# The FFN down projection of a one-core decoder trunk, as four full passes and as seven half-size block products

## The chip, the cores and the metric

The kernel runs on one core of one Trainium2 chip. The metric is the time of one execution on the device, in microseconds (us). The time before is the median of three runs; beside it one execution was recorded by the hardware profiler.

## What is computed

One layer of a decoder trunk on 1024 tokens of width 1024, in float32: a mixing sub-layer with three branches, then a feed-forward sub-layer with a causal convolution of three taps, then a norm. The change is in the last part:

```python
def reference(x, ...):
    h = rms_norm(x, norm_mix[l]);  proj = h @ w_in[l]          # 1024 -> 7184 columns
    ...                                                        # branches a, b, c; gates; w_o
    x = x + merged @ w_o[l]
    h = rms_norm(x, norm_ffn[l])
    a = causal_dwconv(h @ ffn_w_up[l], ffn_conv_w[l]) + ffn_conv_b[l]    # 1024 -> 2 x 2816
    gate, val = jnp.split(a, 2, axis=-1)
    x = x + (jax.nn.silu(gate) * val) @ ffn_w_down[l]                    # 2816 -> 1024
    return rms_norm(x, norm_final)
```

## The kernel before

Every large product runs on TensorE in three matmuls for one: each float32 operand is split into a rounded part `hi` (a ScalarE cast) and a rest `lo` (a subtraction on VectorE or GpSimd), and hi x hi, hi x lo and lo x hi are added up in a PSUM bank of 128x512. In the tiles' names `whi`, `wlo` are weights, `dh`, `dl` the operands of the down projection, `hl` weight operands of the block products, `ah`, `al` their activation operands.

The stages follow one another: norm and first products; the projections (24 blocks); the linear attention and the three branches; `w_o`; the up projection (22 blocks, one for each 128 columns of gate and of value); the down projection with the final norm.

The projections and the up projection already use block products (`Stage`): a block's 2x2 product takes seven products instead of eight, in the order `B11, T1, T2, B22, T3, B21, T4`. The T weights are sums of weight quarters, the S activations sums of activation quarters. A product is 12 matmuls. `prep_right` makes a product's weight operand (line 405 to 416) seven products ahead of its matmuls; `step` moves a finished product from PSUM to the block's tiles `zg` and `zu`, by a ScalarE copy (441 to 445, 453) or a VectorE add (447 to 451). Blocks interleave by one product: the T4 of a block comes after the B11 of the next. The up stage begins with a fill of six blocks (`FILL`), for which B11 and B21 come first.

Side work runs in lanes. `later(delay, step, lane)` puts a step at the end of a lane's queue; `tick` is called after every 3 matmuls (4 ticks a product) and lets each lane's first step go when its delay has passed since the one before. `store_later(delay, out_, in_)` issues a store so many ticks later on SP's queue, `flush` and `flush_stores` run what is left. SP and TensorE keep the order of the program. ScalarE, VectorE and GpSimd are put in order by a planner, which works with modelled times, except in regions marked `manual_schedule`, where they keep the program's order too. All large tiles come from one pool of 52 buffers (`NB`).

After a block's T4, `post_up` applies the taps (ScalarE line 1045, VectorE 1046 and 1048), Silu (1055) and the product with the value half (1057), and stores the tile `tap` to `actd` in HBM.

The down projection runs four passes, for each half of the output columns (`ch`) and of the tokens (`hf`). A pass goes over 11 pairs of blocks (`fp`): an activation pair is loaded from `actd` (`act_pair`, lines 1076 to 1079), weights `dn` by `weights` when `hf` is 0 (162 to 169), and four row blocks take 6 matmuls each. The first two passes also load the residual from `x2d` (`load_residual`) and transpose it on TensorE into `otf` (`residual`, line 1108). `finish` (1121 to 1131) adds the PSUM bank to the residual, sums squares, multiplies with the norm's weight and, in the second half of the columns, scales the rows, which `put_outs` stores. The last three pairs of the last pass run row block by row block.

Of the kernel before, what the change touches and what calls it, by code (L numbers as in the profile page):

```python
# [10 lines left out]
F32 = mybir.dt.float32  # L11
# [5 lines left out]
P = 128  # L17
# [40 lines left out]
def host_layout(inp):  # L58
# [17 lines left out]
    for name in plan():  # L76
# [18 lines left out]
        elif name[:2] == "dn":  # L95
            r, c = int(name[3:]) * 2 * P, int(name[2]) * HALF
            parts.append(kt(w_dn[r:r + 2 * P, c:c + HALF]))
# [22 lines left out]
def trunk_kernel(ctx: ExitStack, tc: tile.TileContext, wst, vec, xt, x, ws, wal, rows, out):  # L120
# [471 lines left out]

    PFILL = 0
# [152 lines left out]

    proj.run(proj_ahead, 2 * PFILL)
# [323 lines left out]
    NP = NF // 2  # L1071

    def act_pair(fp, hf):
        raw = B((P, 2, HALF), name="araw")
        s = slice(hf * HALF, hf * HALF + HALF)
        nc.sync.dma_start(out=raw, in_=actd[2 * fp:2 * fp + 2, :, s].rearrange("f p t -> p f t"))
# [3 lines left out]
        return hi, lo  # L1080

    wdn = {}
    passes = [(0, 0), (0, 1), (1, 0), (1, 1)]
    jobs = [(ch, hf, fp) for ch, hf in passes for fp in range(NP)]
    got = {}

    def fetch(i):
        if i >= len(jobs) or i in got:
            return
        ch, hf, fp = jobs[i]  # L1090
        if hf == 0:
            wdn[ch, fp] = tuple(t.rearrange("p (f c) -> p f c", c=HALF) for t in weights(f"dn{ch}{fp}", 0))
        got[i] = act_pair(fp, hf)
# [24 lines left out]
    def finish(ch, c, ps):  # L1118
        s = slice(ch * HALF, ch * HALF + HALF)
        ot, st = otf[c], fss[:, c]  # L1120
        nc.vector.tensor_tensor(ot[:, s], ps, ot[:, s], op=ALU.add)
        nc.scalar.activation(ps, ot[:, s], AF.Square, accum_out=st[:, ch:ch + 1])
        nc.vector.tensor_tensor(ot[:, s], ot[:, s], nfin[:, s], op=ALU.mult)
        if ch == 0:
            return
# [3 lines left out]
        nc.scalar.activation(ot[:, 0:HALF], ot[:, 0:HALF], AF.Copy, scale=st[:, 2:3])  # L1129
        outs_.append((out[rows_, 0:HALF], ot[:, 0:HALF]))  # L1130
        nc.vector.tensor_scalar(ot[:, HALF:D], ot[:, HALF:D], st[:, 2:3], None, op0=ALU.mult)
        outs_.append((out[rows_, HALF:D], ot[:, HALF:D]))
# [43 lines left out]
    flush_stores()  # L1176

    LAST = 3
    i = 0
    for n, (ch, hf) in enumerate(passes):  # L1180
        banks = [PB() for _ in range(4)]

        def down(j, c, fp):
            w, a = wdn[ch, fp], got[j]
            cs = slice(c * P, c * P + P)
            for q in range(2):
                hi, lo = a[0][:, q, cs], a[1][:, q, cs]
                for e, (l, r) in enumerate(((hi, w[0][:, q]), (hi, w[1][:, q]), (lo, w[0][:, q]))):
                    mm(banks[c], l, r, fp == 0 and q == 0 and e == 0, fp == NP - 1 and q == 1 and e == 2)

        tail = LAST if n == len(passes) - 1 else 0
        for fp in range(NP - tail):
            for a in range(4):
                fetch(i + fp + a)
            if fp == 2:
                put_outs()
            for c in range(4):
                down(i + fp, c, fp)
            got.pop(i + fp)
            if ch == 0 and fp in (1, 3, 5, 7):  # L1200
                load_residual(hf * 4 + fp // 2)
            if ch == 0 and fp in (4, 6, 8, 10):
                residual(hf * 4 + fp // 2 - 2)
        for fp in range(NP - tail, NP):
            fetch(i + fp)
        for c in range(4):
            for fp in range(NP - tail, NP):
                down(i + fp, c, fp)
            finish(ch, hf * 4 + c, banks[c])
            if tail:  # L1210
                put_outs()
        i += NP

# [22 lines left out]
```

## Time and profile before

| | |
|---|---|
| median of 3 runs | 1573.9 us (1572.3 to 1575.32) |
| the profiled execution | 1574.62 us |
| its span, first to last instruction | 1572.9 us |
| TensorE busy | 1530.4 us, 97% of the span |
| mean granted clock of TensorE | 0.986 of full speed |
| VectorE, ScalarE, GpSimd busy | 949.1, 663.2, 404.1 us |
| moved by DMA | 184.08 MB |

The span is that of the profiled execution; the 1.7 us between it and the execution's time lie before the first and behind the last instruction. "Busy" counts time in which an engine has an instruction under way. PE is TensorE, PEld its weight loads, DVE VectorE, ACT ScalarE, POOL GpSimd, SP the queue that issues all DMAs. L424 is line 424 of the kernel.

### The profile page before, as it was taken

To read this page: it belongs to the slowest core of one execution; us is meant where nothing else is said; L and a number is where in the kernel's file an instruction comes from. 1 tells how busy PE (TensorE), PEld (TensorE's weight loads), DVE (VectorE), ACT (ScalarE), POOL (GpSimd) and SP (SyncE) were. 2 spreads that over 40 slices of the span, in tenths; PEclk is the share of its full clock that TensorE was granted. 3 is DMA by queue.
4 is the path that set the end of the run, shared out by engine and by line. 5 is a ranking of instruction groups with operands and counts; after the bars stand their busy time and mean duration, and the time that the engine had idled before them with its cause. 6 is when DMAs were issued, how large, how long until landed. Compare 5 with 4: busy or idle time off the path is not lost.

```text
span 1572.9 us, 18223 instructions
## 1 busy us (share of the span) xinstructions
PE 1530.4 (97%) x7096; PEld 1263.9 (80%) x7096; DVE 949.1 (60%) x1093; ACT 663.2 (42%) x1017; POOL 404.1 (26%) x236
## 2 busy tenths in 40 slices
PE   8899999999999999997999999999999999999998
PEld 8787778888888887875888878888888887888886
DVE  7858776644444442546532698987777775343652
ACT  6634643443343441145122355555444444333341
POOL 5202222222222212015333521222222223302600
PEclk9999999999999999998999999999999999999999
DMA  7223022223323254234424412222222224754341
GB/s 286 94 88 120 36 73 82 93 108 114 114 108 107 81 199 189 91 124 149 145 81 138 157 51 84 94 94 91 92 86 80 81 87 133 275 186 149 121 147 54
DMA packets 74645, 184.08 MB, mean 117 GB/s; under 512 B 6192, under 2 KB 22720, under 8 KB 74560
## 3 DMA queue, kind: packets, MB, share of 16 engines
q1 hardware_dynamic: 74560, 182.93, 33.4%
q8 instruction: 55, 0.90, 0.2%
q14 instruction: 30, 0.25, 0.0%
HBM read 140.96 MB, written 41.94 MB: 116 GB/s over the span
## 4 chain that ended last, share of the span: by engine, by line
PE 83%; issue 7%; DVE 5%; ACT 3%; POOL 1%; DMA 1%; SPq 0%; POOLq 0%; DVEq 0%; ACTq 0%
PE pb L424 48%; PE pb L142 29%; PE pss L142 3%; PE pss L424 2%; DVE hl L416 1%; POOL wlo L169 1%; ACT hl L414 0%; PE pss L1108 0%; DVE al L997 0%; DMA xr<-in_x 0%; DVE raw L409 0%; DVE raw L405 0%; DVE x L1009 0%; DVE raw L411 0%; DVE x L1029 0%
## 5 line engine op out<-in xcount | busy, mean ns | idle before, releaser
L424 PE MATMUL pb<-ah,hl 128*128 128x512 f32 x1856 | 583.3, 391 | 10.1 <-ACT zu L443 5.7
L424 PEld LDWEIGHTS pb<-ah,hl 128*128 128x128 f32 x1856 | 349.9, 189 | 87.7 <-ACT zu L443 6.9
L416 POOL TENSOR_TENSOR hl<-raw,hl 128x512 fp32r<-128x512 f32 x138 | 210.4, 1539 | 651.2 <-ACT hl L414 465.6
L424 PE MATMUL pb<-al,hl 128*128 128x512 f32 x928 | 362.5, 391 | 0.0
L416 DVE TENSOR_TENSOR hl<-raw,hl 128x512 fp32r<-128x512 f32 x184 | 179.0, 981 | 121.1 <-ACT hl L414 118.6
L414 ACT CAST hl<-raw 128x512 fp32r<-128x512 f32 x322 | 186.4, 618 | 125.0 <-DVE raw L407 88.6
L424 PEld LDWEIGHTS pb<-al,hl 128*128 128x128 f32 x928 | 175.0, 189 | 35.9
L169 POOL TENSOR_TENSOR wlo<-raw,whi 128x1024 fp32r<-128x1024 f32 (+1 forms) x50 | 128.7, 2586 | 267.5 <-ACT whi L167 239.3
L424 PE MATMUL pb<-h_hi,hl 128*128 128x512 f32 x576 | 181.7, 389 | 0.0
L142 PE MATMUL pb<-whi,dh 128*128 128x512 f32 x352 | 137.7, 391 | 0.0
L142 PE MATMUL pb<-whi,dl 128*128 128x512 f32 x352 | 137.0, 389 | 0.0
L142 PE MATMUL pb<-wlo,dh 128*128 128x512 f32 x352 | 137.0, 389 | 0.0
L142 PE MATMUL pb<-hi,wlo 128*128 128x512 f32 x320 | 127.1, 397 | 4.1 <-POOL wlo L169 4.1
L142 PE MATMUL pb<-hi,whi 128*128 128x512 f32 x320 | 129.8, 406 | 0.0
L142 PE MATMUL pb<-lo,whi 128*128 128x512 f32 x320 | 127.1, 397 | 0.3 <-DVE lo L229 0.3
L424 PEld LDWEIGHTS pb<-h_hi,hl 128*128 128x128 f32 x576 | 108.1, 188 | 23.2 <-issue 0.8
L1079 DVE TENSOR_TENSOR dl<-araw,dh 128x1024 fp32r<-128x1024 f32 x44 | 82.1, 1895 | 60.5 <-ACT dh L1078 59.1
L424 PE MATMUL pb<-h_lo,hl 128*128 128x512 f32 x288 | 112.0, 389 | 0.0
L142 PEld LDWEIGHTS pb<-whi,dl 128*128 128x128 f32 x352 | 66.1, 188 | 13.9
L142 PEld LDWEIGHTS pb<-whi,dh 128*128 128x128 f32 x352 | 66.1, 188 | 13.5
L142 PEld LDWEIGHTS pb<-wlo,dh 128*128 128x128 f32 x352 | 66.1, 188 | 13.3
L142 PEld LDWEIGHTS pb<-hi,wlo 128*128 128x128 f32 x320 | 61.5, 192 | 17.9 <-POOL wlo L169 4.6
(204 smaller groups left out, 2041.5 us busy)
## 6 DMA issues: line engine op xcount, KB each, us to landing
raw<-in_wst SPq DMA_DIRECT2D x138, 512.0 KB, 4.4
araw<-actd SPq DMA_DIRECT2D x44, 512.0 KB, 5.2
ld<-spd SPq DMA_DIRECT2D x42, 512.0 KB, 4.1
actd<-tap SPq DMA_DIRECT2D x22, 512.0 KB, 2.9
spd<-zg SPq DMA_DIRECT2D x17, 512.0 KB, 2.6
spd<-zu SPq DMA_DIRECT2D x17, 512.0 KB, 3.5
xr<-in_x SPq DMA_DIRECT2D x8, 512.0 KB, 7.7
x<-in_xt SPq DMA_DIRECT2D x16, 256.0 KB, 3.9
```

The costliest lines, as they stand in the source:

```text
L142: nc.tensor.matmul(o, lhsT=l, rhs=r, start=start, stop=stop)
L169: eng.tensor_tensor(lo, raw, f(hi), op=ALU.subtract)
L414: nc.scalar.copy(w[:, 0], t)
L416: eng.tensor_tensor(w[:, 1], t, f(w)[:, 0], op=ALU.subtract)
L424: nc.tensor.matmul(ps, lhsT=l, rhs=r, start=first and k == 0 and i == 0, stop=k == 3 and i == 2, skip_group_check=True)
L1079: nc.vector.tensor_tensor(lo, raw, f(hi), op=ALU.subtract)
```

## The change

The down projection becomes seven block products over all 11 pairs, in the order named above, each with one half of the tokens, one half of the columns and one block of 128 of each pair. Its T weights and S activations are made ahead and pass through HBM. `down_sums` loads the two weight blocks of a pair during the projections, makes four sums on VectorE and stores them to `tsd`; all 22 of its steps are queued in lane 2 before the projections begin. In the up stage, Silu and the product behind it move from `post_up` into `silu`, ten ticks later in a lane of its own (lane 3); every second one calls `act_sums`, four sums on VectorE stored to `ssd`. In the down stage a step loads an activation half and a weight half (`load_step`, six steps ahead), casts and subtracts both at once (`fetch`, four steps ahead), and runs 12 matmuls. VectorE takes all of these subtractions; GpSimd has none. Finished banks are added to the residual after the first step of the next product (`after`), and the whole stage keeps the program's order on all engines. The residual tiles are loaded and transposed within the first product, and the last stores of the up stage wait until its fourth step. The weights lie in HBM as `da` and `db`, one block of 128 rows each.

```diff
-    for ch in range(2):
-        names += [f"dn{ch}{fp}" for fp in range(NF // 2)]
+    for fp in range(NF // 2):
+        names += [f"da{fp}", f"db{fp}"]
...
-    def flush(lanes=(0, 1, 2)):
+    def flush(lanes=(0, 1, 3, 2)):
...
+    tsd = tc.dram_tile([NP, 4, P, HALF], F32, name="tsd")
+    ssd = tc.dram_tile([NP, 4, P, HALF], F32, name="ssd")
...
+    def down_sums(fp):
+        q = {}
+        def fetch_():
+            q["a"], q["b"] = B(name="dqa"), B(name="dqb")
+            for e in "ab":
+                o_ = offs[f"d{e}{fp}"]
+                nc.sync.dma_start(out=q[e], in_=wst[o_:o_ + P * T].rearrange("(p n) -> p n", p=P))
+        def sums():
+            t, u = B((P, 2, HALF), name="dt12"), B((P, 2, HALF), name="dt34")
+            w11, w12, w22, w21 = q["a"][:, left], q["a"][:, rite], q["b"][:, left], q["b"][:, rite]
+            for o_, l, r in ((t[:, 0], w12, w11), (t[:, 1], w22, t[:, 0]), (u[:, 0], w22, w12), (u[:, 1], w21, t[:, 1])):
+                nc.vector.tensor_tensor(o_, l, r, op=ALU.subtract)
+            for i, z in enumerate((t, u)):
+                store_later(16 + 4 * i, tsd[fp, 2 * i:2 * i + 2].rearrange("s p n -> p s n"), z)
+        later(24, fetch_, lane=2)
+        later(16, sums, lane=2)
...
+    for fp in range(NP):
+        down_sums(fp)
     proj.run(proj_ahead, 2 * PFILL)
...
             tg = taps(zg, fi)
-            nc.scalar.activation(tg, tg, AF.Silu)
             tu = taps(zu, NF + fi)
-            nc.vector.tensor_tensor(tg, tg, tu, op=ALU.mult)
-            store_later(14, actd[fi], tg)
+            later(10, lambda: silu(fi, tg, tu), lane=3)
...
+    def silu(fi, tg, tu):
+        nc.scalar.activation(tg, tg, AF.Silu)
+        nc.vector.tensor_tensor(tg, tg, tu, op=ALU.mult)
+        store_later(14 if fi < NF - 2 else 26, actd[fi], tg)
+        pend[fi] = tg
+        if fi % 2:
+            act_sums(fi // 2)
+    def act_sums(fp):
+        one, two = pend.pop(2 * fp), pend.pop(2 * fp + 1)
+        a11, a12, a21, a22 = one[:, left], two[:, left], one[:, rite], two[:, rite]
+        t, u = B((P, 2, HALF), name="as12"), B((P, 2, HALF), name="as34")
+        def put(i, z):
+            store_later(14, ssd[fp, 2 * i:2 * i + 2].rearrange("s p n -> p s n"), z)
+        def first():
+            nc.vector.tensor_tensor(t[:, 0], a21, a22, op=ALU.add)
+            nc.vector.tensor_tensor(t[:, 1], t[:, 0], a11, op=ALU.subtract)
+            put(0, t)
+        def second():
+            nc.vector.tensor_tensor(u[:, 0], a11, a21, op=ALU.subtract)
+            nc.vector.tensor_tensor(u[:, 1], a12, t[:, 1], op=ALU.subtract)
+            put(1, u)
+        later(6, first, lane=2)
+        later(4, second, lane=2)
...
+    jobs = [(m, fp) for m in ORDER for fp in range(NP)]
+    def load_step(i):
+        if i >= len(jobs) or i in raws_:
+            return
+        m, fp = jobs[i]
+        raws_[i] = raw = B((P, 2, HALF), name="araw")
+        a = LEFT[m]
+        if a[0] == "S":
+            nc.sync.dma_start(out=raw[:, 0], in_=ssd[fp, int(a[1]) - 1])
+        else:
+            s = left if a[1] == "1" else rite
+            nc.sync.dma_start(out=raw[:, 0], in_=actd[2 * fp + int(a[2]) - 1, :, s])
+        if m[0] == "T":
+            nc.sync.dma_start(out=raw[:, 1], in_=tsd[fp, int(m[1]) - 1])
+        else:
+            load_down(raw[:, 1], {"B11": f"da{fp}", "B22": f"db{fp}", "B21": f"db{fp}"}[m], int(m == "B21"))
+    def fetch(i):
+        if i >= len(jobs) or i in got:
+            return
+        raw = raws_[i]
         hi, lo = B((P, 2, HALF), F32R, "dh"), B((P, 2, HALF), F32R, "dl")
         nc.scalar.copy(hi, raw)
         nc.vector.tensor_tensor(lo, raw, f(hi), op=ALU.subtract)
+        got[i] = hi, lo
...
-        if n - 1 - i in (8, 6, 4, 2):
-            fetch((9 - n + i) // 2)
+        if n - 1 - i in (14, 10, 7, 5, 3, 1):
+            j = len(raws_)
+            load_step(j)
+            later(9, lambda: fetch(j), lane=1)
+        if n - 1 - i in (4, 2):
+            load_residual(len(xcs))
...
     up.run(up_ahead)
     flush()
-    flush_stores()
...
+    def down(i, c, first):
+        m, fp = jobs[i]
+        hi, lo = got[i]
+        cs = slice(c * P, c * P + P)
+        ps = banks["a" if BANK[m] == "a" else "c"][c]
+        for e, (l, r) in enumerate(((hi, hi), (hi, lo), (lo, hi))):
+            nc.tensor.matmul(ps, lhsT=l[:, 0, cs], rhs=r[:, 1], start=first and fp == 0 and e == 0,
+                             stop=fp == NP - 1 and e == 2, skip_group_check=True)
+    def after(m, c):
+        hf, ch, whole = {"B11": (0, 0, 0), "T1": (1, 1, 0), "T2": (0, 1, 0), "B22": (0, 1, 1), "T3": (1, 1, 1),
+                         "B21": (0, 0, 1), "T4": (1, 0, 1)}[m]
+        add(ch, hf * 4 + c, banks["a" if BANK[m] == "a" else "c"][c])
+        if whole:
+            finish(ch, hf * 4 + c)
+    with tc.manual_schedule(engines={ET.Activation, ET.DVE, ET.Pool}):
+        for n, m in enumerate(ORDER):
+            if m == "T1":
+                banks["c"] = [PB(), PB(), PSS(), PSS()]
+            first = m in ("B11", "T1", "B21")
+            i = n * NP
+            tail = LAST if m == "T4" else 0
+            for fp in range(NP - tail):
+                for a in range(DEPTH + 1):
+                    load_step(i + fp + a)
+                for a in range(DEPTH - 1):
+                    fetch(i + fp + a)
+                if fp in (2, 5):
+                    put_outs()
+                for c in range(4):
+                    down(i + fp, c, first)
+                    if n and fp == 0:
+                        after(ORDER[n - 1], c)
+                got.pop(i + fp)
+                if n == 0:
+                    if fp == 3:
+                        flush_stores()
+                    if 1 <= fp < 7:
+                        load_residual(fp + 1)
+                    if 2 <= fp < 10:
+                        residual(fp - 2)
+        i = n * NP
         for fp in range(NP - tail, NP):
             fetch(i + fp)
         for c in range(4):
             for fp in range(NP - tail, NP):
+                down(i + fp, c, False)
+            after("T4", c)
+            put_outs()
```

`add` adds a bank to `otf`; `finish` keeps the rest of what it did, with its squares written to a buffer `junk` in place of the PSUM bank, and scales the rows after the first half of the columns, which is now the last. `DEPTH` is 6 and `LAST` 3.

## Rows read from the trace of the kernel before

**Rows 1.** The page's head: busy us, share of the span, instructions.

```profile
PE 1530.4 (97%) x7096; PEld 1263.9 (80%) x7096; DVE 949.1 (60%) x1093; ACT 663.2 (42%) x1017; POOL 404.1 (26%) x236
```

**Rows 2.** The page's chain that ended last, by engine.

```profile
PE 83%; issue 7%; DVE 5%; ACT 3%; POOL 1%; DMA 1%; SPq 0%; POOLq 0%; DVEq 0%; ACTq 0%
```

**Rows 3.** Windows of 40 us: busy of PE, PEld, DVE, ACT, POOL; clock; DMA.

```profile
240.00:280.00 40.00, 40.00 (x178) 33.10 (x178) 26.05 (x29) 12.21 (x23) 11.27 (x8) 1.00 0.31 105
...
920.00:960.00 40.00, 37.53 (x156) 29.90 (x155) 37.98 (x41) 23.69 (x34) 13.17 (x6) 0.96 0.17 53
...
1160.00:1200.00 40.00, 40.00 (x178) 33.11 (x177) 32.08 (x34) 18.65 (x28) 10.21 (x7) 1.00 0.23 80
...
1280.00:1320.00 40.00, 38.08 (x161) 31.01 (x160) 27.70 (x28) 21.80 (x29) 13.80 (x6) 0.96 0.39 132
...
1520.00:1560.00 40.00, 40.00 (x178) 33.14 (x177) 9.54 (x14) 6.98 (x11) 0.00 (x0) 1.00 0.12 45
```

**Rows 4.** The chain in order of time, down stage: start, length, what.

```profile
1345.57 0.87 PE pss L1108 x8
...
1445.78 119.71 PE pb L142 x528
```

**Rows 5.** Groups by line and form: busy us, mean ns, idle before.

```profile
L1078 ACT CAST dh<-araw 128x1024 fp32r<-128x1024 f32 x44 | 45.2, 1048 | 14.2 <-DMA araw<-actd 13.2 <-PE pb L142 0.6 <-DMA raw<-in_wst 0.3
...
L169 POOL TENSOR_TENSOR wlo<-raw,whi 128x1024 fp32r<-128x1024 f32 x46 | 122.7, 2678 | 260.8 <-ACT whi L167 239.3 <-PE pb L142 21.3
...
L405 DVE TENSOR_TENSOR raw<-raw 128x512 f32<-128x512 f32 x46 | 31.5, 685 | 49.4 <-POOL hl L416 47.9 <-DMA raw<-in_wst 1.5
...
L411 DVE TENSOR_TENSOR raw<-raw 128x512 f32<-128x512 f32 x46 | 58.0, 1262 | 0.8
```

**Rows 6.** One tile, activations of the down stage: ns min/median/max.

```profile
L1079 DVE TENSOR_TENSOR dl<-araw,dh x44: 1214/1226/3432, 1295.3 to 1524.9; 128x1024 fp32r<-128x1024 f32 x44
```

**Rows 7.** Windows of 5 us at the stage's edge, columns as in rows 3.

```profile
1300.00:1305.00 5.00, 3.66 (x17) 2.69 (x15) 2.79 (x3) 5.00 (x7) 3.65 (x2) 1.00 0.76 213
1305.00:1310.00 5.00, 4.42 (x12) 3.49 (x13) 5.00 (x5) 1.85 (x4) 0.00 (x0) 0.66 0.26 101
...
1335.00:1340.00 5.00, 5.00 (x24) 4.14 (x23) 2.66 (x2) 2.59 (x4) 2.93 (x2) 1.00 1.05 413
```

**Rows 8.** VectorE's timeline at the end: start us, us, operation, idle before.

```profile
1565.51 0.69 DVE L1121 TENSOR_TENSOR ot<-pb,ot 128x512 f32<-128x512 f32 x1 [0.78 <-PE pb L142]
...
1568.32 0.49 DVE L1131 TENSOR_SCALAR ot<-ot,fss 128x512 f32<-128x512 f32 x1
```

**Rows 9.** SP's timeline in the projections and behind the up stage.

```profile
129.16 52.75 SPq L162 DMA_DIRECT2D raw<-in_wst  x6
...
1311.62 16.04 SPq L200 DMA_DIRECT2D actd<-tap  x2
```

**Rows 10.** One tile, the residual: a load's time from issue to landing.

```profile
DMA to landing us min/median/max: 3.7/6.9/10.8
```

**Rows 11.** The chain in order of time at the end of the up stage.

```profile
1300.38 0.95 ACT whi L167
...
1302.79 2.27 ACT tap L1045 x2
```

**Rows 12.** Windows of 10 us early in the projections, columns as in rows 3.

```profile
170.00:180.00 10.00, 7.35 (x26) 5.76 (x25) 8.00 (x10) 6.89 (x11) 2.52 (x2) 0.83 0.00 0
...
190.00:200.00 10.00, 8.62 (x39) 6.79 (x37) 8.99 (x8) 6.37 (x10) 4.24 (x4) 1.00 0.28 106
```

**Rows 13.** Groups by line on VectorE, four up blocks (1160 to 1236).

```profile
L411 DVE TENSOR_TENSOR raw<-raw 128x512 f32<-128x512 f32 x5 | 8.9, 1773 | 0.0
...
L405 DVE TENSOR_TENSOR raw<-raw 128x512 f32<-128x512 f32 x4 | 2.8, 692 | 10.6 <-POOL hl L416 10.6
...
L449 DVE TENSOR_TENSOR zu<-pb,zu 128x512 f32<-128x512 f32 x4 | 2.8, 692 | 2.3 <-PE pb L424 2.3
```

**Rows 14.** One tile, the taps: Silu's durations, first and last start.

```profile
L1055 ACT ACTIVATE tap<-tap x22: 1060/1064/1067, 959.0 to 1324.9; 128x1024 f32<-128x1024 f32 x22
```

More of the change, by code (lines that the diff above doesn't have):

```diff
@@ L94, in host_layout @@
             parts.append(np.stack(two).reshape(2, 4, P, P).transpose(2, 0, 1, 3).reshape(-1))
-        elif name[:2] == "dn":
-            r, c = int(name[3:]) * 2 * P, int(name[2]) * HALF
-            parts.append(kt(w_dn[r:r + 2 * P, c:c + HALF]))
+        elif name[:2] in ("da", "db"):
+            r = int(name[2:]) * 2 * P
+            one, two = w_dn[r:r + P], w_dn[r + P:r + 2 * P]
+            if name[1] == "a":
+                parts.append(one.reshape(-1))
+            else:
+                parts.append(np.concatenate([two[:, HALF:], two[:, :HALF]], axis=1).reshape(-1))
         elif name[0] == "y":
@@ L591, in trunk_kernel, with load_down @@
             e["post"] = post_q if n[0] == "q" else post_k
+    NP = NF // 2
+    tsd = tc.dram_tile([NP, 4, P, HALF], F32, name="tsd")
+    ssd = tc.dram_tile([NP, 4, P, HALF], F32, name="ssd")
+    def load_down(t, name, i):
+        nc.sync.dma_start(out=t, in_=wst[offs[name]:offs[name] + P * T].rearrange("(p s n) -> s p n", p=P, s=2)[i])
+    def down_sums(fp):
[14 more added lines that the diff above has]
+        later(16, sums, lane=2)
     PFILL = 0
@@ L1070, in trunk_kernel @@
     otf = {}
[L1071 to L1076, printed above, removed]
+    junk = B((P, HALF), name="junk")
+    jobs = [(m, fp) for m in ORDER for fp in range(NP)]
+    got = {}
+    raws_ = {}
+    def load_step(i):
[11 more added lines that the diff above has]
+            nc.sync.dma_start(out=raw[:, 1], in_=tsd[fp, int(m[1]) - 1])
+        else:
+            load_down(raw[:, 1], {"B11": f"da{fp}", "B22": f"db{fp}", "B21": f"db{fp}"}[m], int(m == "B21"))
[3 more added lines that the diff above has]
+        raw = raws_[i]
         hi, lo = B((P, 2, HALF), F32R, "dh"), B((P, 2, HALF), F32R, "dl")
@@ L1079, in act_pair @@
         nc.vector.tensor_tensor(lo, raw, f(hi), op=ALU.subtract)
[L1080 to L1093, printed above, removed]
+        got[i] = hi, lo
     xcs = {}
@@ L1116, in put_outs, with add, finish @@
             nc.sync.dma_start(out=o_, in_=i_)
-    def finish(ch, c, ps):
+    def add(ch, c, ps):
+        s = slice(ch * HALF, ch * HALF + HALF)
+        nc.vector.tensor_tensor(otf[c][:, s], ps, otf[c][:, s], op=ALU.add)
+    def finish(ch, c):
         s = slice(ch * HALF, ch * HALF + HALF)
         ot, st = otf[c], fss[:, c]
-        nc.vector.tensor_tensor(ot[:, s], ps, ot[:, s], op=ALU.add)
-        nc.scalar.activation(ps, ot[:, s], AF.Square, accum_out=st[:, ch:ch + 1])
+        nc.scalar.activation(junk, ot[:, s], AF.Square, accum_out=st[:, ch:ch + 1])
         nc.vector.tensor_tensor(ot[:, s], ot[:, s], nfin[:, s], op=ALU.mult)
-        if ch == 0:
+        if ch == 1:
             return
@@ L1128, in finish @@
         rows_ = slice(c * P, c * P + P)
-        nc.scalar.activation(ot[:, 0:HALF], ot[:, 0:HALF], AF.Copy, scale=st[:, 2:3])
+        nc.scalar.activation(ot[:, HALF:D], ot[:, HALF:D], AF.Copy, scale=st[:, 2:3])
+        outs_.append((out[rows_, HALF:D], ot[:, HALF:D]))
+        nc.vector.tensor_scalar(ot[:, 0:HALF], ot[:, 0:HALF], st[:, 2:3], None, op0=ALU.mult)
         outs_.append((out[rows_, 0:HALF], ot[:, 0:HALF]))
-        nc.vector.tensor_scalar(ot[:, HALF:D], ot[:, HALF:D], st[:, 2:3], None, op0=ALU.mult)
-        outs_.append((out[rows_, HALF:D], ot[:, HALF:D]))
     for pair in range(2):
@@ L1175, in trunk_kernel @@
     flush()
-    flush_stores()
     LAST = 3
[L1179 to L1203, printed above, removed]
+    DEPTH = 6
@@ new lines, in trunk_kernel @@
+    banks = {"a": [PB() for _ in range(4)]}
+    def down(i, c, first):
[12 more added lines that the diff above has]
+            finish(ch, hf * 4 + c)
@@ L1207, in trunk_kernel @@
             for fp in range(NP - tail, NP):
[L1208 to L1212, printed above, removed]
+                down(i + fp, c, False)
+            after("T4", c)
+            put_outs()
 _ORDER = ("wst", "vec", "xt", "x", "ws", "wal", "rows")
```

1 line of the change is left out of this document (added).

## The prediction, made before the changed kernel was run

> **What bounds the kernel now.** I read the head of the page first: of the span TensorE is busy 97%, VectorE 60%, ScalarE 42%, GpSimd 26% [rows 1], and by engine the chain of waits is 83% TensorE [rows 2]. So TensorE sets the time unless an edit starves it. The windows of 40 us say where it isn't fed: in the middle of the projections, in the steady up stage and late in the down stage it is busy all 40 us with 178 matmuls, and it loses some at 920 (156 matmuls) and at 1280 (161) [rows 3]. VectorE is the engine to watch: 26 us of 40 in the projections, 38 while the up stage fills, 32 in its steady part, only 9.5 late in the down stage [rows 3]. The chain in order of time gives the pace: 528 matmuls in 119.71 us are 226.7 ns each, and a residual tile's 8 transposes take 0.87 us [rows 4].
>
> **Matmuls removed: -29.9 us.** Before, 4 passes x 11 pairs x 4 row blocks x 6 matmuls = 1056. After, 7 products x 11 x 4 x 3 = 924, of the same shape. 132 x 226.7 ns = 29.9 us. The 64 transposes stay, packed into the first product. A step of the new stage is 12 matmuls, 2.72 us.
>
> **Can that stage be fed?** Each step needs two loads of 256 KB, one cast and one subtraction of 128x1024. The cast takes 1.05 us [rows 5]. The subtraction has a median of 1.23 us and 3.43 at most [rows 6]; before, GpSimd subtracts weights beside it at 2.68 us each [rows 5], and the change leaves GpSimd nothing there. I take 1.23: that and 1.05 are hidden in 2.72 us. The loads come to 0.52 MB in 2.72 us, 193 GB/s; in the burst at 1335 the queue moved 413 GB/s [rows 7]. Nothing is charged; without that cover, a subtraction of 3.43 us would cost 0.7 us a step, 55 in all.
>
> The Trainium skill (DMA: Bandwidth & Descriptors, "Anatomy of one DMA") gives one transfer about 2.0 us fixed plus its bytes at 436 GB/s, fitted on GpSimd's path, and its section on bandwidth wants 1 MiB per transfer. My estimate from it is 2.6 us for 256 KB: 154 loads in a row would need 400 us for a stage of 217. The 413 GB/s were reached with loads of 512 KB that overlap, so here the trace does not bear that reading out.
>
> **Edges of the down stage: +5.8 us.** *Tail.* The last three pairs of the last product run row block by row block. After each block come add, Square, multiply, root, reciprocal, multiply, in the order of the code, on queues that now keep it. One such chain took 3.30 us, from 1565.51 to 1568.81 [rows 8]. A block took 18 matmuls before (4.08 us), longer than the chain, so only the last chain was exposed. It takes 9 now (2.04 us): chains start at the end E - 6.12 and finish at E + 7.1, for E + 3.3. That is +3.8. *Start of the last product.* The four chains of the product before (13.2 us) stand ahead of the subtraction for its sixth step; from 2.0 us ahead of the product they hold VectorE to 11.2 us in it, cast and subtraction end at 13.5, and the step is due at 13.6. A load of the root's table can upset that: +1, between 0 and 2. *First product.* Six residual tiles, the loads, and 2 MB of delayed stores meet in about 37 us: some 11 MB, 290 GB/s. Before, the queue stood 16 us at the store of the last activations [rows 9]; now loads get past it until the fourth step. Residual loads took 6.9 us at the median, 10.8 at most [rows 10], and TensorE's transposes wait in its queue three steps later, about 11 us: +1, between 0 and 4.
>
> **The stall at 1300: -3.** There TensorE was busy only 3.66 us of 5, then ran at a granted clock of 0.66, between its two levels of 1.2 and 2.4 GHz [rows 7]; the chain goes through ScalarE, which casts a down weight (0.95 us) and does two taps (2.27) ahead of a PSUM copy [rows 11]. By the count in the window at 1280, 17 matmuls or 3.9 us were lost [rows 3]. After, the weight casts of that size are gone, six smaller fetches are spread over 14 products, and Silu is queued 10 ticks (2.5 products) later. I take 3 of the 3.9; the bounds are 0 and 3.9.
>
> **Weight sums among the projections: +2.5.** 44 subtractions of 128x512. The nearest rows are the same operation at 0.69 us alone and 1.26 us on average where GpSimd gets in the way [rows 5]: 30 to 55 us of VectorE over 440 ticks (300 us), where it stands idle 14 us of 40 [rows 3]. Hidden in the middle. The first three sets fall before 250 us, where TensorE has stalls already: 26 and 39 matmuls in 10 us where 44 fit [rows 12]. There are also 52 buffers of one size. In the projections I count 28 for activation operands, 6 of the decay, 7 weight operands ahead, 4 raw weights, 4 outputs: 49. The offsets step now stands behind 22 new entries of lane 2, so `lnb` is held some 300 us longer; that and two to four of the sums make 52 to 54. The load queue took 52.75 us there over six loads already [rows 9], and the sums' loads and stores join it. 0 to 8 us.
>
> **Activation sums and the Silu move in the up stage: +2.5.** A block of 7 products is 19.0 us, VectorE busy 15 of it by the window at 1160 [rows 3]. Its idle time is mostly the first weight subtraction waiting 2.65 us for GpSimd (10.6 over four) [rows 13], made 5 or more products ahead of its matmuls, so this time can be used. Added are 2 operations a block: 1.4 us alone, 3.5 if both meet GpSimd as the T4 subtraction does, at 1.77 us [rows 13]. That makes 16.4 to 18.5 of 19.0: full, not over. Two buffers more are held. The fill (920 to 1040) has less room: 38 of 40 us busy at its start [rows 3], and three sets of sums there. 0 to 9 us, most of it in the fill. The order matters as well as the sum: the multiplication after Silu (128x1024, so 1.23 us as in [rows 6]) and four sums can stand ahead of a PSUM add which TensorE needs.
>
> The Trainium skill (SBUF — State Buffer, "Who interferes with whom") says that a VectorE operation with two SBUF inputs and a GpSimd operation that reads SBUF exclude one another for a whole instruction. By it the upper price, 3.5 us a block, would be the usual one. The 1.77 us of [rows 13] bear it out where the two meet; in the same stretch like operations at 0.69 us (the T1 subtraction) did not meet, so I price between them.
>
> **Sum.** -29.9 - 3 + 3.8 + 1 + 1 + 2.5 + 2.5 = -22.1. The profiled execution took 1574.6 us (span 1572.9 and 1.7 around it), 0.7 above the median of the runs: 1552.5, or **1552 us** against the median.
>
> **Rivals.** *A: nothing new is lost and old stalls go.* The Silu move and the new order also close the gaps at 920 (22 matmuls, 5.0 us by [rows 3]) and part of those before 250 [rows 12]: -29.9 - 3.9 - 5 + 3.8 is -35, 1539 us; without any old stall closed beyond 1300 it is 1544. For it: ScalarE no longer waits at the head of its queue for the taps. Against: the stall at 920 lies ahead of the first Silu, at 959 [rows 14]. Chance 0.15, 1536 to 1545. *B: VectorE's queue or the buffers starve TensorE for 10 to 20 us more,* in the fill and at the start of the projections: both upper bounds, 17 us for 5, give 1564; with the edges at theirs, 1571. For it: 38 us of 40, and a load queue that already stands. Chance 0.18. *C, slower:* in every second block of the up stage the planner puts that multiplication and the four sums, slowed by GpSimd to 1.26 us each [rows 5], straight ahead of the add of T3: 1.23 + 4 x 1.26 = 6.3 us. The next matmuls into that bank follow two products later (5.4 us), or one (2.7) where blocks don't interleave. If only 2.7 are there, each pair of blocks loses 3.6 us, 11 pairs 39: the sum without its up-stage term (-24.6) turns to +15, 1589 us. It decides from 2.2 us a pair. Against: the add of T3 usually waits 0.6 us for TensorE, not the reverse [rows 13]. Chance 0.07. *D: loads do not overlap* and the down stage is limited by them: 256 KB at the least landing time of that row, 3.7 us [rows 10], one after another, is 7.4 us a step, 77 steps, 570 us for 217: beyond 1900 us. The 413 GB/s of [rows 7] speak against it. Chance 0.01. It is the Trainium skill's rule above (DMA: Bandwidth & Descriptors, "Anatomy of one DMA") as a mechanism.
>
> **Numbers.** My forecast has 0.55, with its own range 1545 to 1558; A 0.15, B 0.18, C 0.07, D 0.01, and 0.04 for gains and losses that cancel. About 0.2%, 3.1 us, is what a measurement of this kernel can tell from no change. Faster by more than that: 0.55 + 0.15 + 0.17 = 0.87. Within it 0.05, slower 0.08. The range of 8 in 10 takes the forecast, A down to 1541 and B up to 1567.
>
> **What would show it.** Right: about 218 us from the first down matmul to the last with steps of 2.72 us, VectorE under 70% there at 1.23 us a subtraction; no stall at the end of the up stage; four chains of 3.3 us back to back at the end, the last ending some 7 us after the last matmul. Wrong: TensorE waiting on VectorE adds or ScalarE copies every block of the up stage; fewer than 178 matmuls per 40 us in the middle of the projections; transposes or matmuls of the first product waiting for loads; subtractions over 2.7 us in the down stage.

## The result, and the profile after

The changed kernel takes 1552.59 us (median of 4 runs, 1552.16 to 1557.16), the kernel before 1573.36 beside it: a ratio of 0.9868, 95% interval 0.9852 to 0.9884. That is 20.8 us less; 22 had been forecast, to 1552. The profiled execution of the changed kernel, 1557.16 us, lies 4.6 us above the median of its runs, so its stages are compared with their granted clock beside them.

The head of its page, as in [rows 1]:

```profile
PE 1504.3 (97%) x6964; PEld 1240.6 (80%) x6964; DVE 997.2 (64%) x1226; ACT 677.2 (44%) x1028; POOL 346.8 (22%) x214
```

TensorE has 132 matmuls fewer and is 26.1 us less busy, VectorE 48 us more. To see where the span went, both executions are cut where the matmuls change kind: projections, mixing branches, up stage, down stage, and what lies behind the last matmul. Windows of TensorE: stretch, length, busy time and matmuls, granted clock, DMA share and GB/s. First the kernel before:

```profile
115.60:589.50 473.90, 466.36 (x2042) 1.00 0.29 103
589.50:887.50 298.00, 286.73 (x1441) 0.97 0.38 131
887.50:1318.40 430.90, 425.92 (x1866) 0.99 0.26 90
1318.40:1565.50 247.10, 246.84 (x1120) 1.00 0.46 156
1565.50:1572.90 7.40, 0.00 (x0) 0.74 0.37 142
```

The same five stretches of the changed kernel:

```profile
116.90:593.40 476.50, 467.28 (x2042) 1.00 0.45 151
593.40:892.70 299.30, 288.19 (x1440) 0.96 0.39 130
892.70:1327.20 434.50, 426.34 (x1866) 0.99 0.35 121
1327.20:1544.50 217.30, 217.02 (x989) 1.00 0.56 192
1544.50:1555.40 10.90, 0.00 (x0) 0.62 0.38 144
```

Down stage -29.8, tail +3.5, projections +2.6, up stage +3.6; the branches, which the change does not touch, took 1.3 us more at a clock of 0.96 for 0.97, and 1.3 us lie ahead of the projections. So the gain came where it was expected. The up stage is the surprise: -0.5 was forecast. The windows of 40 us, as in [rows 3], say where in it:

```profile
920.00:960.00 40.00, 37.58 (x156) 29.99 (x155) 37.87 (x45) 20.55 (x32) 11.21 (x5) 0.96 0.16 53
1160.00:1200.00 40.00, 40.00 (x178) 33.15 (x177) 33.23 (x40) 18.66 (x28) 9.53 (x6) 1.00 0.31 106
1280.00:1320.00 40.00, 36.28 (x152) 29.24 (x151) 30.39 (x33) 20.26 (x27) 5.08 (x4) 0.96 0.48 160
```

The steady part is full as before, 178 matmuls, with VectorE 1.2 us busier in 40. The end of the stage, which was to lose its stall, has 152 matmuls where [rows 3] have 161: 26 are lost for 17, some 2 us more. By the starts of the matmuls, the last two blocks (168 matmuls) took 44.2 us for 42.1. The other 1.5 us are lost in the fill of six blocks (504 matmuls), which took 122.8 us for 121.3.

The down stage ran as worked out. The subtraction never met GpSimd: 1.22 us each, against the 3.43 at most of [rows 6] (tile view; min, median, max in ns):

```profile
L1164 DVE TENSOR_TENSOR dl<-araw,dh x77: 1210/1216/1227, 1293.3 to 1533.4; 128x1024 fp32r<-128x1024 f32 x77
```

The end: 44 matmuls (from the chain in order of time: start, length, what), then four chains of add, Square, multiply, root, reciprocal, multiply, of which the first two adds stand here (from VectorE's timeline):

```profile
1528.10 10.28 PE pb L1267 x44
...
1538.41 0.69 DVE L1192 TENSOR_TENSOR ot<-pb,ot 128x512 f32<-128x512 f32 x1 [3.80 <-PE pb L1267]
...
1541.67 0.68 DVE L1192 TENSOR_TENSOR ot<-pb,ot 128x512 f32<-128x512 f32 x1
```

The adds follow one another by 3.26 us, while their matmuls are done every 2.04: the chains are the bound there, as forecast.

### The profile page after: what moved, and what is told of

The parts are those of the page before. It is cut to its first block, busy times and chain, and to the rows that moved or that the text cites. A ratio compares the mean times of both kernels' runs of the same rounds, so it can differ in the third digit from the quotient of the medians.

```text
span 1555.4 us, 18426 instructions
## 1 busy us (share of the span) xinstructions
PE 1504.3 (97%) x6964; PEld 1240.6 (80%) x6964; DVE 997.2 (64%) x1226; ACT 677.2 (44%) x1028; POOL 346.8 (22%) x214
## 3 DMA queue, kind: packets, MB, share of 16 engines
q1 hardware_dynamic: 96736, 223.31, 42.1%
## 4 chain that ended last, share of the span: by engine, by line
PE 74%; issue 7%; DVE 5%; ACT 2%; POOL 1%; DMA 0%; SPq 0%; POOLq 0%; ACTq 0%; DVEq 0%
PE pb L428 47%; PE pb L146 12%; PE pb L1267 9%; PE pss L1267 3%; PE pss L428 2%; DVE tap L1080 1%; PE pss L146 1%; POOL wlo L173 1%; DVE tap L1082 0%; PE pss L1180 0%; DVE al L1031 0%; ACT junk L1198 0%; DVE ot L1192 0%; ACT tap L1079 0%; DVE ot L1199 0%
## 5 line engine op out<-in xcount | busy, mean ns | idle before, releaser
L420 POOL TENSOR_TENSOR hl<-raw,hl 128x512 fp32r<-128x512 f32 x138 | 216.0, 1577 | 646.7 <-ACT hl L418 524.4
L420 DVE TENSOR_TENSOR hl<-raw,hl 128x512 fp32r<-128x512 f32 x184 | 158.1, 869 | 79.9 <-ACT hl L418 77.8
L1164 DVE TENSOR_TENSOR dl<-araw,dh 128x1024 fp32r<-128x1024 f32 x77 | 89.3, 1218 | 17.1 <-ACT dh L1163 14.4
L173 POOL TENSOR_TENSOR wlo<-raw,whi 128x1024 fp32r<-128x1024 f32 (+1 forms) x28 | 66.2, 2375 | 149.4 <-ACT whi L171 120.3
L1267 PE MATMUL pb<-dh 128*128 128x512 f32 x242 | 94.9, 392 | 0.0
L1267 PE MATMUL pb<-dl,dh 128*128 128x512 f32 x242 | 94.3, 390 | 0.3 <-DVE dl L1164 0.3
L1267 PE MATMUL pb<-dh,dl 128*128 128x512 f32 x242 | 94.3, 390 | 0.0
L1163 ACT CAST dh<-araw 128x1024 fp32r<-128x1024 f32 x77 | 77.1, 1052 | 31.2 <-PE pb L1267 14.1
L409 DVE TENSOR_TENSOR raw<-raw 128x512 f32<-128x512 f32 x46 | 31.6, 687 | 76.6 <-POOL hl L420 76.6
L445 ACT COPY zg<-pb 128x512 f32<-128x512 f32 x46 | 27.0, 586 | 118.4 <-PE pb L428 108.4
L935 DVE TENSOR_TENSOR ld<-pb,ld 128x512 f32<-128x512 f32 x48 | 32.4, 689 | 69.4 <-PE pb L146 69.3
```

The source lines that it names most:

```text
L173: eng.tensor_tensor(lo, raw, f(hi), op=ALU.subtract)
L409: nc.vector.tensor_tensor(q0, q1, q0, op=ALU.subtract)
L420: eng.tensor_tensor(w[:, 1], t, f(w)[:, 0], op=ALU.subtract)
L445: nc.scalar.copy(zg[:, left], ps)
L935: nc.vector.tensor_tensor(sg[:, s], banks[hf], sg[:, s], op=ALU.mult)
L1267: nc.tensor.matmul(ps, lhsT=l[:, 0, cs], rhs=r[:, 1], start=first and fp == 0 and e == 0, stop=fp == NP - 1 and e == 2, skip_group_check=True)
```

## The experiments

Stages below are cut as above, from the profiled execution of each kernel. Times of one group ran on one chip beside the kernel before (1574.40 us beside the control, the two Silu kernels and the one without weight sums; 1574.50 beside the two of both repairs, the one with loads alone and the one with GpSimd; 1574.18 beside the other four).

**The changed kernel again.**

> The changed kernel unaltered, profiled again. If the stall that is left at the end of the up stage belongs to the order of ScalarE's instructions, it stands again in the same two places (two 10-us stretches near 1290 and 1313 with some 22 matmuls short of 89), whatever the execution; if it was a disturbance of one execution, it is gone and the span is some 5 us shorter. Time 1552.6 +- 1 by either.

1554.79 us, ratio 0.9872 (0.9846 to 0.9898): the time lies 1.2 us above the range that I gave, the ratio is that of the changed kernel. The stall is there again, so it belongs to the program. What TensorE waited for from 1000 us on (in all, times, longest), the kernel before and then this one:

```profile
PE pb L424 <- ACT zu L443: 1.9, 1, 1.9
...
PE pb L428 <- ACT zu L447: 3.7, 2, 1.9
PE pb L428 <- DVE zu L453: 1.4, 1, 1.4
...
```

L443 and L447 are the same copy, of product T1, and its two waits are the stall. L453 is the add of product T3; its wait, which is new, lies in the fill, at 1007 us. ScalarE's timeline at its first half (start, length, instruction, idle time before it and what ended it):

```profile
1283.74 1.25 ACT L1079 ACTIVATE tap<-zg,vecs 128x1024 f32<-128x1024 f32 x1
1284.89 1.23 ACT L1079 ACTIVATE tap<-zu,vecs 128x1024 f32<-128x1024 f32 x1
1286.02 0.60 ACT L418 CAST hl<-raw 128x512 fp32r<-128x512 f32 x1
1286.53 1.06 ACT L1163 CAST dh<-araw 128x1024 fp32r<-128x1024 f32 x1
1288.79 1.06 ACT L1094 ACTIVATE tap<-tap 128x1024 f32<-128x1024 f32 x1 [1.20 <-DVE tap L1082]
1289.75 0.57 ACT L447 COPY zu<-pb 128x512 f32<-128x512 f32 x1
```

L447 copies product T1 out of PSUM, and TensorE waits for it. Ahead of it stand two taps, a weight cast, the cast of the first down operand, 1.20 us of idle time, because Silu's input is not done, and Silu. The queue of [rows 11] is there again, without the down weight's cast, but with Silu. It repeats at 1305 to 1311. Without the down operand ScalarE runs the copy right after the weight cast, and Silu behind the copy of T2 (below, at 1286).

The up stage took 432.8 us here at a clock of 1.00, 434.5 above at 0.99; its last two blocks 42.6 us, for 44.2 above and 42.1 before the change.

**The loads of the first down operands moved.**

```diff
-        if n - 1 - i in (14, 10, 7, 5, 3, 1):
+        if n - 1 - i in (13, 10, 6, 4, 2, 1):
```

> The changed kernel with the loads of the first down operands issued one product earlier or later (at 13, 10, 6, 4, 2 and 1 products before the end in place of 14, 10, 7, 5, 3 and 1), so that their casts do not stand on ScalarE between the taps and the copy of product T1. Theory: the stalls of the last two blocks come from that queue (cast 1.06 us, then Silu held 1.2 to 1.7 us by a VectorE tap, then the copy that TensorE waits for), some 26 matmuls of 226.7 ns are lost there: -4 to -6 us, 1547 to 1549. Rival: VectorE's own backlog at that place holds TensorE, and the stall comes up at the next add: -1 us or less.

1548.46 us, ratio 0.9836 (0.9816 to 0.9855): 5 to 6 us less than the changed kernel by the ratios. The up stage fell from 432.8 to 428.5 us at the same clock, its last two blocks from 42.6 to 38.2, and TensorE's wait for L447 at its end (3.7 us in two) is gone. ScalarE at the same place, now:

```profile
1283.37 0.60 ACT L418 CAST hl<-raw 128x512 fp32r<-128x512 f32 x1
1283.87 0.58 ACT L447 COPY zu<-pb 128x512 f32<-128x512 f32 x1
...
1284.87 1.05 ACT L1163 CAST dh<-araw 128x1024 fp32r<-128x1024 f32 x1
1285.89 0.59 ACT L449 COPY zu<-pb 128x512 f32<-128x512 f32 x1
1286.37 1.07 ACT L1094 ACTIVATE tap<-tap 128x1024 f32<-128x1024 f32 x1
```

The same cast of 1.05 us stands one product later, ahead of the copy of T2, with Silu behind that copy, and costs nothing there. That the order on ScalarE is the cause is shown; what the cast and Silu each cost in it is not separated.

**Silu's step alone, in the kernel before.**

```diff
-            nc.scalar.activation(tg, tg, AF.Silu)
             tu = taps(zu, NF + fi)
-            nc.vector.tensor_tensor(tg, tg, tu, op=ALU.mult)
-            store_later(14, actd[fi], tg)
+            later(10, lambda: silu(fi, tg, tu), lane=3)
...
```

> The kernel before with the Silu step alone queued behind two products; nothing else of the change. Theory: in steady blocks ScalarE ran Silu at that place already (after the copy of product T2), so only the fill blocks and the last two blocks can change: 0, within -2 to +2 us of the kernel before (1573). Rival: the queued Silu is what frees the products, and the gain of the whole change contains some us of it: -4 us or more. Second rival: it costs the up stage what the changed kernel lost there (+3.6 us of the up stage): +3 us.

1573.95 us, ratio 1.0002 (0.9987 to 1.0018): nothing. In steady blocks the planner had put Silu behind the copy of T2 already. The trace shows two changes that offset each other. The fill took 122.9 us for 121.3, and TensorE waits once for the add of T3 (here L449), as in the changed kernel:

```profile
PE pb L424 <- DVE zu L449: 1.6, 1, 1.6
```

The last two blocks took 38.9 us for 42.1: TensorE's wait for the copy of T1 is 0.4 us there and the clock does not fall. Silu stands behind that copy in both kernels, so it is not Silu itself that left its way; which step of the new order did it is not traced.

**Silu back at its old place, in the changed kernel.**

```diff
-            later(10, lambda: silu(fi, tg, tu), lane=3)
+            silu(fi, tg, tu)
```

> The changed kernel with Silu issued at once after the taps, as before the change; the sums of activations as in the change. Theory: 1552.6 -2 to +2, because the place of Silu on ScalarE in steady blocks is the same either way; at the end of the up stage the stalls of some 3 us each stay. Rival: the stalls at the end of the up stage come from the queued Silu, and go with it: 1547 to 1549.

1559.77 us, ratio 0.9903 (0.988 to 0.9925): 5 us slower than the control beside it by the medians, 3 by the two profiled executions, where I expected nothing. Both expectations fail. The up stage took 437.0 us, 4.2 more than the control's. The last two blocks have about 1 of it (43.5 us for 42.6); most of the new loss lies at the end of the fill. Windows of 10 us there, this kernel and then the control:

```profile
1010.00:1020.00 10.00, 10.00 (x46) 1.00 0.12 52
1020.00:1030.00 10.00, 8.31 (x36) 1.00 0.32 126
1030.00:1040.00 10.00, 8.88 (x40) 1.00 0.42 139
```

```profile
1010.00:1020.00 10.00, 9.36 (x42) 1.00 0.18 71
1020.00:1030.00 10.00, 10.00 (x46) 1.00 0.35 102
1030.00:1040.00 10.00, 10.00 (x46) 1.00 0.56 214
```

12 matmuls net, 2.7 us. ScalarE holds Silu there until VectorE's tap, which takes 2.31 us beside a subtraction on GpSimd, is done, with the copy behind it:

```profile
1020.27 1.06 ACT L1094 ACTIVATE tap<-tap 128x1024 f32<-128x1024 f32 x1 [2.66 <-DVE tap L1082]
1021.24 0.57 ACT L447 COPY zu<-pb 128x512 f32<-128x512 f32 x1
```

VectorE then runs the four activation sums, with one weight subtraction between them, ahead of the weight differences and of the add of T3. TensorE waits 1.6 us for the copy and 2.6 us in three for that add; the control has 1.4 us in one, for the add. So beside the sums the queued Silu is worth 2.7 us at this place and 4.2 in the up stage; by itself it gave nothing. The rest of the 5 is not traced.

**Without the sums of activations** (the products read activations in their place).

```diff
-        if fi % 2:
-            act_sums(fi // 2)
...
```

> The changed kernel without the sums of activations: no 48 VectorE operations and no 24 stores behind the Silu step; the products with S1 to S4 in the down stage read a half of the activations in place of the sums, so their values are wrong and their bytes the same. Theory: steady blocks have the VectorE time to spare, so only the fill of the up stage (which lost 1.8 us) and the end of it can gain: -1 to -3 us, 1549.6 to 1551.6. Rival: VectorE is near its limit all through the up stage and the sums cost 0.3 us or more in each of 22 blocks: -6 us or more, 1546 or less. Second rival: nothing, 1552.6 +- 0.5.

1554.06 us, ratio 0.9867 (0.9846 to 0.9887): nothing. Its up stage took 436.3 us at a clock of 0.99, the changed kernel's 434.5 at 0.99; the fill 122.9 us, with them 122.8. The sums are free. The wait for the add of T3 in the fill is there without them too (1.6 us), as it is with Silu's step alone: it came with that step. In steady blocks of the changed kernel (groups by line on VectorE, mean ns, idle before), as in [rows 13]:

```profile
L1118 DVE TENSOR_TENSOR as<-tap 128x512 f32<-128x512 f32 x2 | 3.6, 1778 | 0.0
...
L453 DVE TENSOR_TENSOR zu<-pb,zu 128x512 f32<-128x512 f32 x4 | 2.7, 684 | 0.0
```

One sum of four takes 1.78 us, with a GpSimd subtraction under way beside it; three take 0.68. The Trainium skill (SBUF — State Buffer, "Who interferes with whom") has a VectorE operation with two SBUF inputs and a GpSimd operation that reads SBUF exclude one another for a whole instruction. The trace agrees at that one sum, and it is one in four. The add of T3 (L453) no longer waits for TensorE, as it did for 2.3 us in four blocks [rows 13]: the slack that rival C was about is used up, and TensorE does not wait yet in these blocks.

**Without the sums of weights** (the products T1 to T4 read weights in their place).

```diff
-    for fp in range(NP):
-        down_sums(fp)
...
-            nc.sync.dma_start(out=raw[:, 1], in_=tsd[fp, int(m[1]) - 1])
+            load_down(raw[:, 1], f"da{fp}", 0)
```

> The changed kernel without the sums of the down weights: none of the twelve loads, 48 VectorE subtractions and stores in the projections; the products T1 to T4 of the down stage read the left half of the first row tile of the weights in place of the sums, so their values are wrong and their bytes the same. Theory: the sums are all that the projections lost: time 1552.6 - 2.6 = 1550.0, the projections 474.1 us as before. Rival: the projections' 2.6 us is clock and noise of one execution: 1552.6 +- 0.5, the projections 476 again. Second rival: loads of the sums or their stores disturbed the weights' stream: as the first, but with the load landings of the projections shorter.

1551.80 us, 3.0 less than the control beside it, with a wide interval (ratio 0.9817 to 0.9879); the projections 473.9 us, as in the kernel before, for 476.4. The theory holds. (The change has 22 loads and 44 subtractions in the projections, and 44 sums of activations, not twelve and 48 as the expectations count them.)

**The weights loaded and stored, but not subtracted.**

```diff
-            t, u = B((P, 2, HALF), name="dt12"), B((P, 2, HALF), name="dt34")
...
-                nc.vector.tensor_tensor(o_, l, r, op=ALU.subtract)
+            t, u = (q[e].rearrange("p (s n) -> p s n", s=2) for e in "ab")
```

> The changed kernel in which the down weights are loaded in the projections and stored again as they are, without the 48 VectorE subtractions (the output is wrong; the transfers and their bytes are the change's). Theory: VectorE's subtractions are what the projections pay for, ScalarE's casts and the copies that TensorE waits for stand behind them: projections 473.9 us as without loads and sums. Rival: the transfers disturb the stream of weights or its buffers: 476.5 us as in the change.

1552.82 us, ratio 0.986 (0.9832 to 0.9887), the projections 475.6 us: 1.7 of the 2.6 are left, so the theory fails in the main. The 0.9 that went with the subtractions, and with their result buffers, which this edit leaves out as well, stood at 218 us in the control. One place of the rest is to be seen on ScalarE. In this kernel, and in the control alike, the gate's L517 stands ahead of the copy of T1; in the kernel with late weight sums (two experiments on), and before the change, behind it. First this one, then the one with late sums:

```profile
172.92 1.05 ACT L517 ACTIVATE cum<-cum 128x1024 f32<-128x1024 f32 x1
173.87 0.56 ACT L447 COPY zu<-pb 128x512 f32<-128x512 f32 x1
```

```profile
172.90 0.58 ACT L447 COPY zu<-pb 128x512 f32<-128x512 f32 x1
...
173.90 1.06 ACT L517 ACTIVATE cum<-cum 128x1024 f32<-128x1024 f32 x1
```

That is 1 us: TensorE's next matmul starts 4.1 us after the one before it, for 3.0 before the change. The planner's order changed with instructions that ScalarE doesn't even run. A second place is at 237 us, in this kernel and in the control: there the copy of T1 leaves ScalarE idle for 1.45 us until a subtraction on VectorE (L420) is done, and TensorE loses 0.5 us; before the change it does not wait there. What ties the copy to that subtraction is not traced.

**The last norm skewed by one block.** The reciprocal, scaled copies and stores of a block come behind the next one's add and Square.

```diff
         nc.scalar.activation(junk, ot[:, s], AF.Square, ...)
+        if ch == 0:
+            scale_out()
         nc.vector.tensor_tensor(ot[:, s], ot[:, s], nfin[:, s], op=ALU.mult)
...
```

> The changed kernel with the last norm skewed: the reciprocal, the scaled copies and stores of a column block stand behind the add and the Square of the next one. Theory: the four finishes of product T4 stand in a chain of 3.26 us each behind the last matmuls, and run at the pace of 2.2 to 2.5 us when two overlap, so the tail after the last matmul goes from 10.9 to 7 or 8 us: -3 to -4 us, 1548.6 to 1549.6. Rival: the two engines are busy all through the 3.26 us, and only idle time inside the chain is moved: -1 us or less.

1550.40 us, ratio 0.9852 (0.9831 to 0.9873): 2.5 to 3 us less than the changed kernel by the ratios, for 3 to 4 expected. By the stages it is 3.7. The tail goes from 10.9 to 7.8 us (the theory had 7 or 8) and the down stage from 217.3 to 216.7: the wait at the start of the last product is gone as well. The adds then follow one another by 2.2 us (shown with the next kernel).

**Both repairs, and the weight sums begun late.** The second kernel adds to the first:

```diff
-        later(24, fetch_, lane=2)
+        later(24 if fp else 180, fetch_, lane=2)
```

> The changed kernel with both repairs: the first down operands' loads moved and the last norm skewed. Theory: the stall at the end of the up stage and the tail are different places, so the gains add: up stage 428.5 us as with the loads moved alone, down stage 216.7 and tail 7.8 us as with the skew alone; 4.3 + 3.7 = 8 us less than the changed kernel, 1544.5 to 1546. Rival: the up stage's end and the down stage's start share the buffers, and part of one gain is lost: 1548.

> The kernel with both repairs, and the first sum of the down weights begins 180 steps of four matmul groups into the projections in place of 24. Theory: the projections lose their 2.6 us only in their first 120 us, where VectorE and ScalarE still catch up; later the sums are covered: projections 473.9 to 474.5 us, whole 2 to 2.6 us less than with the two repairs, 1542 to 1543.5. Rival: the sums cost the same wherever they stand: projections 476.5.

Both repairs: 1543.88 us, ratio 0.9805 (0.9785 to 0.9826); up stage 428.5, down stage 216.7, tail 7.8: the gains add. The first two adds of its last product on VectorE, 2.22 us apart:

```profile
1526.49 0.69 DVE L1192 TENSOR_TENSOR ot<-pb,ot 128x512 f32<-128x512 f32 x1 [6.42 <-PE pb L1281]
...
1528.71 0.69 DVE L1192 TENSOR_TENSOR ot<-pb,ot 128x512 f32<-128x512 f32 x1
```

With the late sums: 1542.17 us, ratio 0.9793 (0.9774 to 0.9812), the fastest kernel here, though the two intervals do not tell its 1.7 us from none. Its projections took 472.3 us. Some 1.8 of the 4.2 saved there are the clock, an estimate (0.09 of 20 us): it was 1.00 between 160 and 180 us where the control had 0.91. What is left is 2.4: sums that begin 110 us later (at 260.8 us for 150.4; the delay is 156 groups of three matmuls) cost nothing. `lnb` is held 102 us longer still, so it is no cause; whether the sums' own buffers are one in the first 120 us is not shown.

**Two products more in the down stage** (T1 and T2 twice).

```diff
+    DOWN = ("B11", "T1", "T2", "T1", "T2", "B22", "T3", "B21", "T4")
...
```

> The changed kernel with products T1 and T2 of the down stage done twice (nine block products for seven, eight of the old cost plus one; the output is wrong, T1 and T2 are added twice). Theory: TensorE alone sets the pace of the down stage, so 2 x 132 more matmuls at 226.7 ns: +59.9 us, 1612.5 (1611 to 1614). Rival: the products with sums from HBM are held by loads or by the splits on ScalarE and VectorE, and cost more than their matmuls: +62 us or more. Second rival: they cost less than their matmuls at this pace, because the clock of this stage was not full: +57 or less.

1614.74 us, 0.7 above the range expected; the stage itself comes out as expected. The down stage by its window, with the columns as above:

```profile
1325.70:1602.80 277.10, 276.80 (x1252) 1.00 0.57 192
```

277.1 - 217.3 = 59.8 us for 264 matmuls, 226.5 ns each. TensorE alone sets the pace; two loads of 256 KB, a cast and a subtraction for each step are free.

**A third of the down stage's subtractions on GpSimd.**

```diff
-                    fetch(i + fp + a)
+                    fetch(i + fp + a, nc.gpsimd if (i + fp + a) % 3 == 2 else None)
...
```

> The changed kernel with every third of the down stage's subtractions on GpSimd in place of VectorE. Theory: a step has 2.72 us of matmuls and VectorE only 1.22 us of work for it, and the splits run five steps ahead, so also a subtraction of 2 to 4 us on GpSimd and longer ones on VectorE beside it are covered: down stage 217.3 +- 0.5 us, no wait of TensorE for dl but the one at the start of T4. Rival: the splits run close to their need, and the slower ones hold TensorE at 26 steps: +5 us or more in the down stage.

1555.19 us in one execution; the down stage 218.5, +1.2, where 0.5 was the bound. Groups of the stage: VectorE's subtraction now takes 1.88 us, GpSimd's 2.84:

```profile
L1164 DVE TENSOR_TENSOR dl<-araw,dh 128x1024 fp32r<-128x1024 f32 x49 | 89.3, 1878 | 22.0 <-ACT dh L1163 19.3 <-DMA araw<-tsd 2.4 <-DMA araw<-in_wst 0.3
...
L1164 POOL TENSOR_TENSOR dl<-araw,dh 128x1024 fp32r<-128x1024 f32 x23 | 65.2, 2843 | 165.7 <-ACT dh L1163 161.2 <-DVE dl L1164 4.5
```

TensorE waited once, 1.5 us, behind the finish chains, at the sixth step of the last product; the changed kernel waits there too, 0.6 us. So the cover is as wide as the prediction had it, and the one place where it is thin is the one that it named.

## Why the prediction was right, and where it was not

*Matmuls and the stage's feed: right.* -29.9 forecast; with the two edge terms inside the stage (+1 and +1) -27.9; measured -29.8. Of the edges, the residual tiles cost nothing: their loads took 6.8 us at the median, 7.7 at most. The wait at the last product's start is 0.6 us, what the skew takes out of the stage. The loads do overlap; a window of 5 us in the first product:

```profile
1360.00:1365.00 5.00, 5.00 (x28) 4.21 (x27) 2.59 (x3) 3.75 (x5) 0.00 (x0) 1.00 1.06 406
```

406 GB/s with loads of 256 KB, TensorE full: rival D falls. With it falls the reading of the Trainium skill's figure of about 2.0 us fixed for a transfer (DMA: Bandwidth & Descriptors, "Anatomy of one DMA"; fitted on GpSimd's path) as a price that is paid for each one in turn.

*Tail: right.* +3.8 forecast, +3.5 measured, by the mechanism named.

*Weight sums: right in size, half right in cause.* +2.5 forecast, +2.6 measured, lost in the first 120 us, as located. I gave VectorE's time and the buffers as causes. The subtractions, with their result buffers, make 0.9 of it; 1.7 stay with the transfers alone. Of these, 1 us is a ScalarE instruction that the planner moved ahead of a copy, and 0.5 a copy that waits for VectorE at 237 us; the last 0.2 is not traced, and whether buffers are behind the 0.5 is not shown.

*The stall at 1300: wrong.* This is the step that failed: "After, the weight casts of that size are gone, six smaller fetches are spread over 14 products, and Silu is queued 10 ticks (2.5 products) later. I take 3 of the 3.9". The reading of the chain behind it [rows 11] left out a row: between the weight cast and the taps stood the cast of a down operand, which the change keeps.

```profile
1301.32 0.94 ACT dh L1078
```

So only one of two such casts left the queue ahead of the copy of T1. Silu, which stood behind that copy here before the change, stands ahead of it now, and the queue holds the copy up in two blocks for one. The term is +2, not -3: the last two blocks took 44.2 us for 42.1 (42.6 in the control, whose clock did not fall). The gain was there to be had: with the casts moved by one product they took 38.2, nearly all of the 3.9 less than before the change.

*Activation sums and Silu's move: +2.5 forecast, +1.5 measured, in the fill, as located, but not by the sums.* The sums fit into time that VectorE waited for GpSimd, as the text argued; I then charged the fill for them all the same. What the fill lost came with Silu's step: the one wait for the add of T3 is there with that step alone and without the sums. Why the step makes that add late is not traced.

That the sum came out so near is in part luck. The stall's error of 5 us is offset by 1 in the fill and 2 at the edges: -22.1 forecast, -29.8 + 3.5 + 2.6 + 3.6 = -20.1 in the profiled execution, -20.8 by the medians. Of the rivals, A's further gains did not come, since the stall at 920 stands as it was (156 matmuls). B and C name waits that are there, but small: 2.6 us in the projections, and 1.4 us once at the add of T3, in the fill, none in steady blocks. (With the bounds that it names, B's last figure is 1552 + 12 + 4 = 1568; 1571 takes the stall's bound of 0 as well.)

## What to carry to other kernels

A copy out of PSUM that frees TensorE's next bank is the instruction to guard on an in-order engine. Count what stands ahead of it, in the new order, before calling a stall gone: removing one entry of that queue and adding another gains nothing. Moving casts of 1.05 us by one product gave back 4.3 us, a seventh of what the 132 matmuls gave, and one stretch of the engine's timeline showed it. Where a chain of short instructions on two engines is repeated and exposed, interleaving two of its turns (3.26 to 2.2 us a turn) gave back 3.7 us.

## What the runs showed of the hardware that was not expected

The same stall can cost more in one execution than in another. In the profiled execution of the changed kernel and in that of the control TensorE was busy 3.14 of 5 us at the same point of the program; then it was granted 0.70 of its clock in one and all of it in the other. Windows of 5 us, the changed kernel and then the control:

```profile
1290.00:1295.00 5.00, 3.14 (x14) 0.96 0.00 0
1295.00:1300.00 5.00, 5.00 (x18) 0.70 0.52 172
```

```profile
1286.00:1291.00 5.00, 3.14 (x15) 1.00 0.00 0
1291.00:1296.00 5.00, 5.00 (x24) 1.00 0.27 88
```

18 matmuls for 24: 1.4 us more for one stall, at a granted clock between the levels of 1.2 and 2.4 GHz. TensorE's idle time was 1.86 us in both. Eight profiled executions here have this pair of stalls, and each block comes in two lengths: the first took 21.2 us in two of them and 22.8 in six, the second 21.4 in three and 23.0 in five. So a fall of the clock adds 1.6 us to a stall of 1.9, or nothing. The times of one kernel go the same way, though that it is this loss alone is not shown: of the kernel before, the shortest span, 1568.5 us, had a mean clock of 0.989 and the longest, 1581.5, one of 0.978. Taking a stall away takes this loss away too, which a sum of durations does not hold.
